# A due date for the readers of PSUM, more tiles for split weights, and a stricter VectorE in the planner of a two-layer block

## The chip, the cores and the metric

One core of one Trainium2 chip runs the whole program. The metric is device microseconds (us) of one execution; the figure for a kernel is the median of its runs. "The profile" is the page written from one profiled execution, "the trace" the record behind it, from which further rows can be asked.

## The reference

Two layers of a block that mixes tokens in four ways at once. There are 256 latent tokens and 256 context tokens of width 1024; layer 0 computes both, layer 1 the latent ones alone (its context tokens serve only as keys and values).

```python
for l in range(DEPTH):
    h = modulate(rms_norm(x, norm_gain[l, 0]), mod[:, 0], mod[:, 1])
    hc = modulate(rms_norm(ctx, norm_gain[l, 0]), mod_c[:, 0], mod_c[:, 1])
    pl = split_cols(h @ w_in[l])
    pc = split_cols(hc @ w_in[l])
    a_l, a_c = gqa_branch(...)
    b_l, b_c = retention_branch(...)
    c_l, c_c = mla_branch(...)
    d_l, d_c = diff_branch(...)
    y = gated_merge([a_l, b_l, c_l, d_l], pl[13], w_branch[l], w_out[l])
    x = x + mod[:, 2][:, None] * y
    h2 = modulate(rms_norm(x, norm_gain[l, 1]), mod[:, 3], mod[:, 4])
    x = x + mod[:, 5][:, None] * swiglu(h2, w_ffn_in[l], w_ffn_out[l])
    ...
```

`mod` comes from a matrix of 1024 by 6144 weights for each layer (`adaln`). `gated_merge` sums, over the branches, sigmoid gates times the branch's projection, and projects the sum once more. `swiglu` has 2816 hidden channels. All is float32.

## The kernel before

**The arithmetic.** Every matmul against weights, and most of the attention, is made of three: each operand is split into a high part rounded to fp32r and a low part, the rest, and the products hi·hi, hi·lo and lo·hi are summed in PSUM. For weights, `Weights._split` takes a piece of a loaded tile `wraw`, copies it to `whi` (`cp`, a CAST), and VectorE subtracts: `wlo = wraw - whi`. The same pair of steps splits the transposed probabilities (`pthi`, `ptlo`, out of the PSUM tile `ps_t`), stacked queries and keys (`sthi`, `stlo`), normalised activations (`hhi`, `hlo`) and branch outputs (`ohi`, `olo`).

**The stages** in the order of time: modulation of the first norm and transposes of the input; layer 0's input projection, with its four branches' attention laid between its matmuls; layer 0's merge (gates, branch projections and output projection); its FFN; the same for layer 1. The modulation vectors of later stages are summed on VectorE (`macc`: one weight row block times a column of `sil`, added on, in chains of SCALAR_TENSOR_TENSOR) beside the earlier stages; `MODS` says beside which. In the merge `glog` and `sig` hold the gates; `glog<-glog,ps_s` multiplies a gate into a branch projection that stands in PSUM, and frees that PSUM bank. In the FFN, `fsig` does the same for silu(gate) times up.

**The order.** Nothing is emitted directly. A `Recorder` collects every operation with what it depends on, and `schedule` plans them with a cost for each: `backward` places every operation as late as it may go, which gives its priority `prio` (the lowest first); `forward` goes through time and lets each engine take, among its ready operations, the one of lowest `prio` that `allowed` admits. `emit` (line 432) then issues all of them in that order, so that all rows of the trace bear one line. Engines work through their own lists strictly in order: an operation that waits holds up all behind it on that engine.

Three rules of `forward` matter here. `allowed` refuses an operation whose new tiles would exceed a limit: 8 banks of PSUM, by uses `PS_LIMITS = {"acc":5,"s":8,"t":3,"v":3}`; 73 tiles in the pool "u"; and of these at most `W_LIMIT = 34` for `whi` and `wlo`, 17 pairs (`w_tiles`, line 536). The priority does not know PSUM: an operation that would free a bank counts by when its result is wanted. And `worth` decides between engines where an operation has alternatives: `cp` (line 576) is ScalarE's first and may go to VectorE; `scale_rows` (line 580) is VectorE's first and may go to ScalarE or GpSimd. An engine that is not the first takes the operation only if it would end it sooner than the other, with a margin added to its own end:

```python
if e != ops[i][0][0][0]:
    mine += MARGIN[e]
```

With -0.3 for VectorE it takes a copy even if it would end it up to 0.3 us (of the planner's time) later than ScalarE.

Of the kernel before, what the change touches and what calls it, by code (L numbers as in the profile page):

```python
# [33 lines left out]
WRAW_LIMIT = 4  # L34
MRAW_LIMIT = 4
SLACK = 1
MARGIN = {"vector": -0.3, "scalar": -0.1, "gpsimd": 0}
W_LIMIT = 34
MOD_LAG = 600
REL_LAG = 200  # L40
DECAY_LAG = 0
# [22 lines left out]
class Recorder:  # L64
# [221 lines left out]
    def forward(self, users, deps, prio):  # L286
        ops = self.ops
        n = len(ops)
        tiles = {}
        caps = {}  # L290
        for nm, (f, l, c) in self.span.items():
            tiles[nm] = [[tag for tag, _ in self.tag[nm]], f, l, c, False]
            caps.update(self.tag[nm])
        prof = {t: np.zeros(n + 1, dtype=np.int32) for t in caps}
        for tags, f, l, c, _ in tiles.values():
            for tag in tags:
                prof[tag][f:l + 1] += 1
        live = dict.fromkeys(caps, 0)
        for t, c in caps.items():
            assert prof[t].max() <= c, (t, prof[t].max(), c)  # L300
        done = [False] * n
        issued = [False] * n
        low = 0
        free = dict.fromkeys(self.ENGINES, 0.0)
        left = [len(d) for d in deps]
        est = [0.0] * n
        pick = [0] * n
        heaps = {e: [] for e in self.ENGINES}
        ends = []
        wait = [(est[i], i) for i in range(n) if not left[i]]  # L310
        heapq.heapify(wait)
        now = 0.0
        order = []
        self.times = {}

        held = 0.0

        def begin(v):
            return max(now, held) if v[6] else now

        def allowed(i):
            new = {}
            for nm in ops[i][2]:
                t = tiles[nm]
                if not t[4]:
                    for tag in t[0]:
                        new.setdefault(tag, []).append(t[1])
            for tag, firsts in new.items():
                k = len(firsts)
                if live[tag] + k > caps[tag]:  # L330
                    return False
                f = max(firsts)
                if f > low and prof[tag][low:f].max() + k > caps[tag] - (SLACK if caps[tag] > 16 else 0):
                    return False
            return True

        def worth(e, i, p):

            mine = next(begin(v) + v[4] for v in ops[i][0] if v[0] == e)
            if e != ops[i][0][0][0]:  # L340
                mine += MARGIN[e]
            for v in ops[i][0]:
                if v[0] != e:
                    t = max(begin(v), free[v[0]]) + v[4]
                    if t < mine:
                        t += sum(ops[j][0][0][4] for q, j in heaps[v[0]] if (q, j) < (p, i) and not issued[j])
                        if t < mine:
                            return False
            return True
        while len(order) < n:  # L350
            while wait and wait[0][0] <= now + 1e-9:
                _, i = heapq.heappop(wait)
                for v in ops[i][0]:
                    heapq.heappush(heaps[v[0]], (prio[i], i))
            while ends and ends[0][0] <= now + 1e-9:
                _, i = heapq.heappop(ends)
                done[i] = True
                for nm in ops[i][2]:
                    t = tiles[nm]
                    t[3] -= 1  # L360
                    if t[3] == 0:
                        for tag in t[0]:
                            live[tag] -= 1
                            prof[tag][low:t[2] + 1] -= 1
                while low < n and done[low]:
                    low += 1
            nxt = wait[0][0] if wait else 1e18
            if ends:
                nxt = min(nxt, ends[0][0])
            for e in self.ENGINES:  # L370
                h = heaps[e]
                while h and issued[h[0][1]]:
                    heapq.heappop(h)
                if not h:
                    continue
                if free[e] > now + 1e-9:
                    nxt = min(nxt, free[e])
                    continue
                skipped = []
                found = -1  # L380
                while h and len(skipped) < 200:
                    p, i = heapq.heappop(h)
                    if issued[i]:
                        continue
                    if allowed(i) and (len(ops[i][0]) == 1 or worth(e, i, p)):
                        found = i
                        break
                    skipped.append((p, i))
                for x in skipped:
                    heapq.heappush(h, x)  # L390
                if found < 0:
                    continue
                i = found
                issued[i] = True
                for nm in ops[i][2]:
                    t = tiles[nm]
                    if not t[4]:
                        t[4] = True
                        for tag in t[0]:
                            live[tag] += 1  # L400
                            if t[1] > low:
                                prof[tag][low:t[1]] += 1
                pick[i] = next(x for x, v in enumerate(ops[i][0]) if v[0] == e)
                v = ops[i][0][pick[i]]
                end = begin(v) + v[4]
                free[e] = end
                if v[6]:
                    held = end
                self.times[i] = now
                if e == "sync":  # L410
                    free[e] = max(end, now + 0.565)
                heapq.heappush(ends, (end + (DMA_LAT if e == "sync" else 0.0), i))
                order.append(i)
                for u in users[i]:
                    left[u] -= 1
                    w = ops[u][0][0][0]
                    lat = 0.0 if e == "tensor" == w else v[5] + self.EXTRA[w]
                    est[u] = max(est[u], end + lat)
                    if not left[u]:
                        heapq.heappush(wait, (est[u], u))  # L420
                nxt = min(nxt, free[e])
            if nxt >= 1e18:
                raise RuntimeError("schedule stuck")
            now = max(now, nxt)
        return order, pick
# [89 lines left out]
class Builder:  # L515
# [20 lines left out]
    def w_tiles(self):  # L536
        pair = self.u(F32R, "whi"), self.u(F32R, "wlo")
        for t in pair:
            self.nc.own(t, ("u", NU), ("w", W_LIMIT))
        return pair  # L540
# [1724 lines left out]
```

## Time and profile before

| what | value |
|---|---|
| runs | 1776.82, 1778.41, 1778.12 us; median 1778.12 |
| profiled execution | 1776.79 us |
| its span, by the trace | 1774.9 us (1.9 us lie outside it) |
| TensorE busy | 1726.4 us, 97% of the span |
| VectorE busy | 1334.3 us, 75% |
| ScalarE busy | 846.9 us, 48% |
| GpSimd busy | 58.7 us, 3% |
| mean granted clock of TensorE | 0.993 of full speed |

PE is TensorE's matmuls, PEld its weight loads, DVE is VectorE, ACT ScalarE, POOL GpSimd, SP the engine that issues most transfers. In a row `out<-in` names the tiles; numbers of buffers are left out. "Idle before" is the time that an engine stood still ahead of an instruction, with what released it. Matmul durations overlap their neighbours; what one costs is the distance from its start to the next start.

### The profile page before, as it was taken

What the parts mean: (1) busy time and instruction counts of PE and PEld (TensorE: products, weight loads), DVE (VectorE), ACT (ScalarE), POOL (GpSimd) and SP (SyncE); (2) the same over time, 40 slices, a digit from 0 to 9 for tenths busy, and PEclk for the clock granted to TensorE, in tenths of its full rate; (3) what the DMA queues carried; (4) which work ended last, traced back from release to release, by engine and by line L of the source; (5) the groups of instructions that cost most, each with busy time, mean ns of one, the idle gap of its engine ahead of it and who ended that gap; (6) DMA issues with size and microseconds to landing.
All of it is one profiled execution on the core that took longest, in us unless ns stands there. A gap on an engine that the chain in (4) does not pass through costs nothing. (4 is left out here: it accounts for less than half of the span.)

```text
span 1774.9 us, 30925 instructions
## 1 busy us (share of the span) xinstructions
PE 1726.4 (97%) x11510; PEld 1564.5 (88%) x11510; DVE 1334.3 (75%) x3055; ACT 846.9 (48%) x2014; POOL 58.7 (3%) x89
## 2 busy tenths in 40 slices
PE   7999999999899999999999999998999899999999
PEld 5988999998687887878888789997999789999999
DVE  5899999888989678786436533989989796786563
ACT  4378665556423333532222322666655544564441
POOL 0010000001010000000000000000000100000000
PEclk9999999999999999999999999999999999999999
DMA  9413113334546465355226522342234576756451
GB/s 310 165 45 117 50 35 110 93 96 125 166 154 193 151 214 166 108 189 189 83 72 197 189 89 75 110 118 63 72 93 129 148 222 190 233 161 183 138 187 62
DMA packets 204345, 243.72 MB, mean 137 GB/s; under 512 B 9994, under 2 KB 183204, under 8 KB 204196
## 3 DMA queue, kind: packets, MB, share of 16 engines
q1 hardware_dynamic: 203840, 241.61, 44.4%
q8 instruction: 90, 1.47, 0.3%
q14 instruction: 59, 0.48, 0.1%
q10 hardware_dynamic: 356, 0.14, 0.0%
HBM read 224.15 MB, written 1.05 MB: 127 GB/s over the span
## 5 line engine op out<-in xcount | busy, mean ns | idle before, releaser
L432 ACT CAST whi<-wraw 128x512 fp32r<-128x512 f32 (+3 forms) x630 | 361.1, 605 | 353.6 <-PE ps_acc L432 160.3
L432 DVE TENSOR_TENSOR wlo<-wraw,whi 128x512 fp32r<-128x512 f32 (+4 forms) x674 | 436.4, 668 | 120.2 <-PE ps_acc L432 65.7
L432 PE MATMUL ps_acc<-hhi,wlo 128*128 128x256 f32 (+1 forms) x864 | 292.7, 339 | 8.9 <-DVE wlo L432 6.1
L432 PE MATMUL ps_acc<-hlo,whi 128*128 128x256 f32 (+1 forms) x864 | 289.7, 335 | 0.2
L432 PE MATMUL ps_acc<-hhi,whi 128*128 128x256 f32 (+1 forms) x864 | 289.4, 335 | 0.0
L432 PE MATMUL ps_acc<-whi,hhi 128*128 128x256 f32 (+2 forms) x896 | 262.5, 293 | 1.2 <-ACT x L432 0.9
L432 PE MATMUL ps_acc<-wlo,hhi 128*128 128x256 f32 (+2 forms) x896 | 254.5, 284 | 0.3 <-DVE wlo L432 0.3
L432 PE MATMUL ps_acc<-whi,hlo 128*128 128x256 f32 (+2 forms) x896 | 254.6, 284 | 0.0
L432 PEld LDWEIGHTS ps_acc<-hhi,wlo 128*128 128x128 f32 x864 | 164.6, 191 | 28.4 <-DVE wlo L432 7.7
L432 PEld LDWEIGHTS ps_acc<-hlo,whi 128*128 128x128 f32 x864 | 164.6, 190 | 17.3 <-DVE hlo L432 0.7
L432 PEld LDWEIGHTS ps_acc<-hhi,whi 128*128 128x128 f32 x864 | 164.7, 191 | 14.9
L432 PEld LDWEIGHTS ps_acc<-whi,hhi 128*128 128x128 f32 x896 | 171.2, 191 | 3.0 <-ACT x L432 1.3
L432 PEld LDWEIGHTS ps_acc<-wlo,hhi 128*128 128x128 f32 x896 | 171.4, 191 | 1.0 <-DVE wlo L432 0.5
L432 PEld LDWEIGHTS ps_acc<-whi,hlo 128*128 128x128 f32 x896 | 171.0, 191 | 0.0
L432 DVE SCALAR_TENSOR_TENSOR macc<-mraw,sil,macc 128x512 f32<-128x512 f32 x224 | 157.8, 752 | 15.7 <-DMA mraw<-in_w_mod_dram 13.4
L432 PE MATMUL ps_acc<-fhi,wlo 128*128 128x256 f32 (+1 forms) x396 | 127.5, 322 | 0.0
L432 PE MATMUL ps_acc<-flo,whi 128*128 128x256 f32 (+1 forms) x396 | 126.2, 319 | 0.0
L432 PE MATMUL ps_acc<-fhi,whi 128*128 128x256 f32 (+1 forms) x396 | 126.1, 319 | 0.0
L432 PE MATMUL ps_s<-hhi,wlo 128*128 128x512 f32 (+1 forms) x352 | 119.2, 339 | 1.3 <-ACT hhi L432 1.3
L432 PE MATMUL ps_s<-hlo,whi 128*128 128x512 f32 (+1 forms) x352 | 119.1, 338 | 0.5 <-DVE hlo L432 0.5
L432 PE MATMUL ps_s<-hhi,whi 128*128 128x512 f32 (+1 forms) x352 | 119.0, 338 | 0.0
L432 PE MATMUL ps_s<-ohi,wlo 128*128 128x512 f32 (+1 forms) x256 | 88.4, 345 | 6.7 <-DVE glog L432 6.6
(247 smaller groups left out, 3563.5 us busy)
## 6 DMA issues: line engine op xcount, KB each, us to landing
wraw<-in_w_in_dram SPq DMA_DIRECT2D x124, 512.0 KB, 4.6
mraw<-in_w_mod_dram SPq DMA_DIRECT2D x96, 512.0 KB, 4.8
wraw<-in_w_ffn_in_dram SPq DMA_DIRECT2D x88, 512.0 KB, 3.5
wraw<-in_w_ffn_out_dram SPq DMA_DIRECT2D x40, 512.0 KB, 4.6
wraw<-in_w_branch_dram SPq DMA_DIRECT2D x32, 512.0 KB, 3.6
wraw<-in_w_out_dram SPq DMA_DIRECT2D x16, 512.0 KB, 4.9
stb<-sthi SPq DMA_DIRECT2D x36, 128.0 KB, 2.3
std<-stlo SPq DMA_DIRECT2D x24, 128.0 KB, 2.3
```

What stands on the lines that cost most here:

```text
L432: getattr(getattr(self.nc, eng), m)(*a, **k)
```

## The change

Three parts, all in the planner; no operation is added or removed.

1. **A due date.** In `forward`, an operation that is not TensorE's and touches a tile in PSUM is a `reader`. When it becomes ready, its priority becomes the smaller of its own and the time at which it became ready plus `DUE = 12.0` us (on the scale of the priorities, `horizon` being the start of the backward plan).
2. **More tiles for split weights.** `W_LIMIT` goes from 34 to 40, that is from 17 to 20 pairs, out of the same 73.
3. **VectorE's margin** goes from -0.3 to 0.3: it takes a copy of ScalarE's only where it would end it more than 0.3 us sooner.

```diff
-MARGIN = {"vector": -0.3, "scalar": -0.1, "gpsimd": 0}
-W_LIMIT = 34
+DUE = 12.0
+MARGIN = {"vector": 0.3, "scalar": -0.1, "gpsimd": 0}
+W_LIMIT = 40
...
         held = 0.0
+        prio = list(prio)
+        horizon = -min(prio)
+        reader = [o[0][0][0] != "tensor" and any(x.startswith("ps_") for x in o[2]) for o in ops]
...
             while wait and wait[0][0] <= now + 1e-9:
                 _, i = heapq.heappop(wait)
+                if reader[i]:
+                    prio[i] = min(prio[i], est[i] - horizon + DUE)
                 for v in ops[i][0]:
                     heapq.heappush(heaps[v[0]], (prio[i], i))
```

What the planner emits with it, at three places. The emitting line is 432 before and 438 in the changed kernel; "x3" is three in a row.

**Place 1: VectorE at the start of layer 0's merge** (around 479 us of the trace). `macc` are sums of modulation vectors, `glog<-glog,ps_s` the readers of PSUM. Before:

```order
L432 TENSOR_TENSOR wlo<-wraw,whi 128x512
L432 SCALAR_TENSOR_TENSOR macc<-mraw,sil,macc 128x512 x3
L432 TENSOR_TENSOR wlo<-wraw,whi 128x512
L432 SCALAR_TENSOR_TENSOR macc<-mraw,sil,macc 128x512 x8
L432 SCALAR_TENSOR_TENSOR glog<-glog,ps_s 128x512 x3
L432 TENSOR_TENSOR glog<-glog 128x512
L432 TENSOR_TENSOR wlo<-wraw,whi 128x512
L432 SCALAR_TENSOR_TENSOR glog<-glog,ps_s 128x512 x2
```

Eight `macc` stand ahead of the first reader. In the changed kernel:

```order
L438 SCALAR_TENSOR_TENSOR glog<-glog,ps_s 128x512
L438 TENSOR_TENSOR olo<-o,ohi 128x512
L438 SCALAR_TENSOR_TENSOR glog<-glog,ps_s 128x512
L438 TENSOR_TENSOR wlo<-wraw,whi 128x512
L438 TENSOR_TENSOR olo<-o,ohi 128x512
L438 TENSOR_TENSOR wlo<-wraw,whi 128x512
L438 TENSOR_TENSOR olo<-o,ohi 128x512 x3
L438 TENSOR_TENSOR wlo<-wraw,whi 128x512
L438 SCALAR_TENSOR_TENSOR glog<-glog,ps_s 128x512
L438 TENSOR_TENSOR olo<-o,ohi 128x512
L438 SCALAR_TENSOR_TENSOR glog<-glog,ps_s 128x512
L438 TENSOR_TENSOR wlo<-wraw,whi 128x512 x4
```

The first four readers of the merge stand ahead of the run of `macc`, which begins with the next row.

**Place 2: VectorE in layer 1's attention of the GQA branch** (around 1205 us), with the numbers of the tiles. `mk` are normalised keys of another branch, which touch no PSUM; `ptlo`, `o` and `v` read PSUM. Before:

```order
L432 TENSOR_TENSOR mk_2825<-x_3087,sm_3093 128x4x64
L432 CAST pthi_3072<-ps_t_3071 128x512
L432 TENSOR_TENSOR mk_2827<-x_3087,sm_3093 128x4x64
L432 TENSOR_TENSOR ptlo_3073<-ps_t_3071,pthi_3072 128x512
L432 TENSOR_TENSOR mk_2829<-x_3088,sm_3093 128x4x64
L432 TENSOR_TENSOR mk_2831<-x_3088,sm_3093 128x4x64
```

VectorE casts `pthi_3072` itself, and `mk` stand between. In the changed kernel:

```order
L438 TENSOR_TENSOR ptlo_3073<-ps_t_3071,pthi_3072 128x512
L438 TENSOR_TENSOR o_2933<-ps_v_3036,pvl_3037 64x256
L438 TENSOR_TENSOR t2_3048<-x_3040,ropeg_2727 128x512
L438 TENSOR_TENSOR v_3151<-ps_acc_3110,v_3151 128x4x64
L438 TENSOR_TENSOR ptlo_3076<-ps_t_3074,pthi_3075 128x512
L438 TENSOR_TENSOR v_3152<-ps_acc_3110,v_3152 128x4x64
L438 CAST pthi_3083<-ps_t_3082 128x512
```

`pthi_3072` has gone to ScalarE, and the readers of PSUM follow one another with the `mk` behind them. Over the program VectorE's `pthi<-ps_t` casts of 128x512 go from 33 to 7, its `x<-ps_acc` copies of 128x512 from 12 to 3, its `sthi<-ps_t` of 128x512 from 12 to 8, and its `whi<-wraw` casts of 128x512 from 30 to 48, ScalarE having the rest; GpSimd's `p<-p,sm` of 128x512 go from 7 to 14. TensorE has the same instructions as before.

**Place 3: TensorE in layer 0's attention of the GQA branch** (around 150 us). `ps_acc<-whi,cqhi` and its two companions are projections of another branch; `ps_t<-ident,p` transposes probabilities, `ps_v` multiplies them into the values, `ps_s` are scores. Before:

```order
L432 MATMUL ps_v<-pthi,v 128x256
L432 MATMUL ps_acc<-whi,cqhi 128x256
L432 MATMUL ps_acc<-wlo,cqhi 128x256
L432 MATMUL ps_acc<-whi,cqlo 128x256
L432 MATMUL ps_v<-ptlo,v 64x256 x2
L432 MATMUL ps_v<-pthi,v 128x256
L432 MATMUL ps_t<-ident,p_583 128x128 x4
L432 MATMUL ps_acc<-whi,cqhi 128x256
```

Projections stand between the steps of the attention. In the changed kernel:

```order
L438 MATMUL ps_v<-pthi,v 128x256
L438 MATMUL ps_t<-ident,p_583 128x128
L438 MATMUL ps_v<-ptlo,v 64x256 x2
L438 MATMUL ps_v<-pthi,v 128x256
L438 MATMUL ps_s<-sthi 128x512
L438 MATMUL ps_s<-stlo,sthi 128x512
L438 MATMUL ps_s<-stb 128x512
L438 MATMUL ps_s<-std,stb 128x512
L438 MATMUL ps_t<-ident,p_585 128x128 x4
```

Here 57 matmuls of the attention follow one another without a projection.

## Rows read from the trace of the kernel before

**Rows 1.** The page's first part: busy time, share of the span, instructions.
```profile
PE 1726.4 (97%) x11510; PEld 1564.5 (88%) x11510; DVE 1334.3 (75%) x3055; ACT 846.9 (48%) x2014; POOL 58.7 (3%) x89
```

**Rows 2.** Windows: stretch, its us, busy PE PEld DVE ACT POOL, granted clock, DMA.
```profile
100.00:175.00 75.00, 73.09 (x490) 64.67 (x489) 70.67 (x176) 62.42 (x162) 8.45 (x20) 1.00 0.34 96
175.00:450.00 275.00, 270.91 (x2111) 260.36 (x2111) 251.39 (x656) 173.95 (x443) 15.17 (x20) 1.00 0.29 83
...
725.00:775.00 50.00, 47.19 (x282) 39.43 (x281) 44.69 (x103) 23.29 (x85) 0.00 (x0) 1.00 0.44 138
775.00:1175.00 400.00, 400.00 (x2125) 343.04 (x2124) 219.03 (x454) 136.51 (x322) 8.99 (x16) 1.00 0.40 125
1175.00:1300.00 125.00, 117.37 (x873) 108.71 (x872) 119.36 (x297) 89.51 (x200) 4.53 (x4) 0.99 0.26 75
...
1375.00:1450.00 75.00, 64.46 (x470) 61.21 (x469) 62.97 (x174) 36.59 (x86) 5.24 (x10) 0.93 0.53 160
```

**Rows 3.** Timelines of DVE, then of PE, about 480 us; then windows.
```profile
478.85 5.39 DVE L432 SCALAR_TENSOR_TENSOR macc<-mraw,sil,macc 128x512 f32<-128x512 f32 x8
484.15 1.88 DVE L432 SCALAR_TENSOR_TENSOR glog<-glog,ps_s 128x512 f32<-128x512 f32 x3
...
484.89 0.79 PE L432 MATMUL ps_s<-ohi,wlo 128*128 128x512 f32 x1 [5.32 <-DVE glog L432]
...
484.90:488.50 3.60, 3.60 (x9) 2.83 (x10) 3.60 (x7) 0.62 (x1) 0.00 (x0) 0.50 0.58 154
575.00:600.00 25.00, 25.00 (x112) 20.71 (x111) 16.50 (x26) 5.92 (x10) 3.24 (x3) 1.00 0.45 141
```

**Rows 4.** Waits of PE, 1375 to 1450 us (total, times, longest); then windows.
```profile
PE ps_acc L432 <- DVE wlo L432: 5.5, 3, 2.5
...
PE ps_s L432 <- DVE glog L432: 1.3, 1, 1.3
...
1375.00:1400.00 25.00, 21.59 (x164) 20.82 (x162) 16.81 (x44) 10.72 (x19) 1.77 (x6) 0.93 0.29 77
1400.00:1425.00 25.00, 19.26 (x139) 17.62 (x140) 24.13 (x68) 14.94 (x38) 3.48 (x4) 0.97 0.70 220
```

**Rows 5.** Waits of PE, 1175 to 1300 us; then a window.
```profile
PE ps_v L432 <- DVE o L432: 2.7, 1, 2.7
PE ps_t L432 <- DVE ptlo L432: 2.4, 3, 1.9
...
1200.00:1225.00 25.00, 19.19 (x119) 15.92 (x118) 23.69 (x70) 13.72 (x34) 0.00 (x0) 0.93 0.08 22
```

**Rows 6.** Waits of PE, 100 to 450 us.
```profile
PE ps_t L432 <- DVE otok L432: 0.9, 1, 0.9
PE ps_t L432 <- DVE x L432: 0.8, 1, 0.8
```

**Rows 7.** Timeline of DVE about 762 us; then waits of PE, 725 to 775 us.
```profile
762.20 11.34 DVE L432 SCALAR_TENSOR_TENSOR macc<-mraw,sil,macc 128x512 f32<-128x512 f32 x17
...
PE ps_acc L432 <- DVE fsig L432: 1.3, 1, 1.3
```

**Rows 8.** Groups of instructions by form, DVE, ACT, POOL: busy us, mean ns.
```profile
L432 DVE CAST pthi<-ps_t 128x512 fp32r<-128x512 f32 x33 | 22.5, 684 | 2.8 <-PE ps_t L432 2.6
...
L432 DVE CAST whi<-wraw 128x512 fp32r<-128x512 f32 x30 | 12.6, 420 | 8.3 <-DMA wraw<-in_w_in_dram 4.8 <-PE ps_acc L432 3.5
...
L432 DVE TENSOR_TENSOR mk<-x,sm 128x256 f32<-128x256 f32 x16 | 6.1, 412 | 0.0
...
L432 DVE TENSOR_SCALAR p<-p,sm 128x512 f32<-128x512 f32 x24 | 11.5, 478 | 0.2
...
L432 ACT CAST whi<-wraw 128x512 fp32r<-128x512 f32 x578 | 340.9, 620 | 340.9 <-PE ps_acc L432 149.8 <-PE ps_s L432 56.3 <-DMA wraw<-in_w_in_dram 41.5
...
L432 ACT CAST pthi<-ps_t 128x512 fp32r<-128x512 f32 x67 | 38.5, 586 | 17.2 <-PE ps_t L432 13.1 <-PE ps_v L432 3.1 <-DVE o L432 0.4
...
L432 POOL TENSOR_TENSOR p<-p,sm 128x512 f32<-128x512 f32 x7 | 7.7, 1101 | 136.1 <-DVE sm L432 136.1
```

## The prediction

> **What bounds the kernel now.** I read the page's first part, then windows by stage, then the waits of TensorE in the stages that are not full, then the timeline around each. TensorE is busy in 1726.4 of 1774.9 us [rows 1]; 48.5 us are idle. Where it is full, as from 775 to 1175 us (400.00 of 400.00) [rows 2], nothing that the planner does for VectorE can gain, since TensorE's work is the same before and after. So the question is only where the 48.5 us lie and who holds them. Five stretches have them: 100 to 175 lacks 1.9, 175 to 450 lacks 4.1, 725 to 775 lacks 2.8, 1175 to 1300 lacks 7.6, 1375 to 1450 lacks 10.5 [rows 2]; and one wait by itself, 5.32 us at 479 us [rows 3]. The other 16 us (48.5 less these 32.2) are spread over the other stages, the start and the end among them, and are left as they are. In all six places the waits name VectorE most, with a reader of PSUM (`glog`, `o`, `ptlo`, `fsig`) or a `wlo`. VectorE is also the busy one there: 70.67 of 75 us, 119.36 of 125 [rows 2].
>
> A wait costs a second time. After the 5.32 us, nine matmuls of 512 columns took 3.60 us at a granted clock of 0.50, that is at 1.2 instead of 2.4 GHz; at full clock 112 of the same take 25.00 us [rows 3], 0.223 each, so nine take 2.0: 1.6 us were lost. TensorE had stood still before the clock fell.
>
> **The sum.** All terms are against the profiled execution, 1776.8 us. The median of the runs is 1.3 above it, and 1.3 is added at the end. About 0.2%, 3.5 us, is what a measurement of this kernel can tell from no change.
>
> *(a) The merge of layer 0.* Eight `macc` take 5.39 us on VectorE from 478.85, and the `glog` that frees a bank starts at 484.15, when TensorE has stood still for nearly as long [rows 3]. In the new order (place 1) the first four `glog` stand ahead of the run. The wait goes with its clock: 5.3 + 1.6 = **-6.9** (at least 5, if another 1.9 us of `wlo` or `olo` stay ahead of it). What is late next is `macc`, which no stage near it wants.
>
> *(b) 1375 to 1450.* Three waits for `wlo` make 5.5 us and one for `glog` 1.3 [rows 4]. VectorE has less to do ahead of them: 26 casts `pthi` of 684 ns (17.8 us) and 9 copies `x`, taken at the same price (6.2 us), leave it over the program, while 18 casts `whi` of 420 ns (7.6 us) come to it [rows 8]; the PSUM readers go by their due date, and 20 pairs let `wlo` be made earlier. I take both waits as gone, and the clock of the two windows that hold the `wlo`, (0.07 + 0.03) × 25 = 2.5 us [rows 4]: **-9.3**. At most all goes: 10.5 of idle time and 0.07 × 75 = 5.2 of clock [rows 2], -15.7. At least nothing goes.
>
> *(c) 1175 to 1300.* Waits for `o` 2.7 and `ptlo` 2.4, the longest 1.9, and a window of 25 us at 0.93, which costs 1.75 [rows 5]. Place 2 shows four `mk` of 412 ns [rows 8] that stood between the readers of PSUM and now stand behind, and the cast on ScalarE. I take 2.7 + 1.9 + 1.75 = **-6.3**; at most 7.6 + 1.75 = -9.4, at least nothing.
>
> *(d) 100 to 450.* 6.0 us are idle in many waits of under 1 us. Of these `otok` 0.9 and `x` 0.8 are VectorE's work behind PSUM [rows 6]: **-1.7**, between 0 and -6.0.
>
> *(e) 725 to 775.* Seventeen `macc` in a row take 11.34 us ahead of `fsig`, and TensorE waits 1.3 for it [rows 7]. The due date lifts `fsig` over them: **-1.3**, between 0 and -2.8.
>
> *(f) Work that moves.* ScalarE gets the 35 copies, at 586 each 20.5 us, and gives up 18 casts of 620, 11.2 [rows 8]; it is at 48% [rows 1], so this costs nothing while its idle time covers it. SP issues the same transfers, and the tiles that a delayed `macc` holds come free some 5 us later, and no wait of TensorE read here names a transfer [rows 3 to 7]: nothing, and if the cover were gone, some of (g).
>
> *(g) New waits.* No row shows what the readers' precedence pushes back: `mk`, `macc`, scalings of `p`. GpSimd gets 7 more of `p`, at 1101 ns against VectorE's 478 [rows 8], and if TensorE waited for each, 7 × 0.62 = 4.4. The upper bound is two more stretches like 1200 to 1225, where 5.8 us are idle and 1.75 lost to the clock [rows 5]: 15.1. Below nothing is left out, since the gains are counted above. I take **+4**, by the nearer row.
>
> -6.9 - 9.3 - 6.3 - 1.7 - 1.3 + 4 = -21.5. 1776.8 - 21.5 = 1755.3, and with 1.3 the median is **1757**.
>
> **The rivals.**
>
> *Slower: the fillers are used up too early.* With 20 pairs and earlier readers the projections run ahead of the attention, and nothing is left to lay between its steps: place 3 shows 57 matmuls of layer 0's GQA attention without a projection. TensorE then goes at the pace of VectorE's and ScalarE's chain from scores to `ptlo`, as from 1200 to 1225 us [rows 5]. Two such stretches, one in each layer, cost 15.1. If then only (a), (e) and the longest `wlo` wait of 2.5 [rows 4] are gained, 10.7, the sum is +4.4: 1776.8 + 4.4 + 1.3 = 1782.5. It decides from about 14 us of new waits on with these gains. For it: VectorE has only 4.3 us free of 75 in that stage of layer 0 [rows 2]. Against: it is VectorE that loses work there, and TensorE had 1.9 us idle with the same chain.
>
> *No effect.* A due date of 12 us after becoming ready is longer than the waits that it should remove (5.32 at most) [rows 3], so most readers keep the place that they had, and what is gained in one place is lost in (g): within 3.5 us, 1778. Against: place 1 shows the readers moved.
>
> *ScalarE becomes the bound.* From 100 to 175 us it is busy for 62.42 of 75 [rows 2], 12.6 free. If all 35 copies fell there, 20.5 - 12.6 = 7.9 us would be over, and the forecast would become 1757 + 8 = 1765. The Trainium skill has a rule that speaks against the third part: "TensorEngine Tiling (Array Packing)", section "PSUM Bottleneck", says that the copying out of PSUM can become the limit and that ScalarE and VectorE should both be used for it. By that rule the 26 casts should stay shared; no row here shows TensorE waiting long for ScalarE. Only a part of the 35 lies in that stage, and a cast from PSUM takes VectorE 684 ns and ScalarE 586, while one from SBUF takes 420 against 620 [rows 8]: the exchange of the two kinds makes both engines cheaper.
>
> *Better than forecast.* Everything that (a) to (e) bound goes and nothing comes: 6.9 + 15.7 + 9.4 + 6.0 + 2.8 = 40.8, so 1736.0, and 1737 with 1.3. It asks that no stage be limited by VectorE any more, though it stays at 119.36 less some 10 of 125 [rows 2]. Half of the step from the forecast to it gives 1747.
>
> **How the numbers follow.** Forecast (1747 to 1767) 0.55; ScalarE the bound, which is still faster, 0.15; better than 1747, 0.10; no effect 0.10; slower 0.10. So faster by over 0.2% (below 1774.6) 0.80, within it 0.10, slower (above 1781.7) 0.10. The range is 1740 to 1776: downwards it takes in most of "better", upwards all the cases of (g) in which new waits take nearly all of the gain; it leaves out the slower case, most of no effect and the last of "better".
>
> **What the profile would show.** If right: no wait for `glog` of over 1 us in layer 0's merge and no 0.5 clock behind it (a); `wlo` waits between 1375 and 1450 under 1 us together (b); `o` and `ptlo` gone from the waits about 1206 and 1219 us (c); VectorE busy for about 1318 us (1334.3 - 17.8 - 6.2 + 7.6), ScalarE for about 856 (846.9 + 20.5 - 11.2); TensorE idle for some 27 us rather than 48.5. It would be wrong if waits for `ps_t` or `ps_v` of over 5 us together stood in either GQA attention (the fillers), if they named ScalarE's `pthi` (ScalarE the bound), or if new waits stood where `macc`, `mk` or `p` are wanted, in stretches that are full now.

## The result, and the profile after

The changed kernel takes 1749.99 us (median of 4 runs, 1748.84 to 1751.57); beside it the kernel before took 1777.47 (4 runs). The ratio is 0.9846, with a 95% interval of 0.9829 to 0.9863: 27.5 us faster, where 21.5 had been forecast. The profiled execution took 1750.57 us, its span is 1748.5, against 1774.9 before: 26.4 less.

The first part of the page of the changed kernel answers to [rows 1]:

```profile
PE 1716.3 (98%) x11510; PEld 1559.5 (89%) x11510; DVE 1313.7 (75%) x3020; ACT 857.7 (49%) x2041; POOL 70.5 (4%) x97
```

TensorE's idle time went from 48.5 to 32.2 us (1748.5 - 1716.3), 16.3 less. The other 10.1 us are in its busy time, 1726.4 before, for the same 11510 matmuls. About 7 of them go with the granted clock, whose mean rose from 0.993 to 0.997 (worked out in the last section); what the other 3 are is not shown. VectorE lost 20.6 us and ScalarE gained 10.8.

Windows of the changed kernel, in the columns of [rows 2]; two are moved along with the work, which comes some 10 and 25 us earlier there:

```profile
100.00:175.00 75.00, 73.69 (x502) 65.76 (x501) 68.38 (x176) 65.58 (x168) 10.41 (x21) 1.00 0.34 95
175.00:450.00 275.00, 273.36 (x2118) 262.03 (x2117) 245.29 (x648) 178.49 (x453) 17.09 (x23) 1.00 0.31 86
715.00:765.00 50.00, 45.56 (x272) 39.13 (x271) 44.82 (x103) 26.08 (x91) 1.09 (x1) 0.97 0.40 131
1175.00:1300.00 125.00, 122.75 (x940) 114.97 (x939) 123.16 (x300) 94.82 (x215) 9.58 (x8) 1.00 0.28 83
1350.00:1425.00 75.00, 68.78 (x531) 66.50 (x530) 64.92 (x199) 44.17 (x112) 5.09 (x10) 0.95 0.49 142
```

Four of the five are fuller than their rows before; the FFN's norm of layer 0 (715 to 765) is emptier: 4.4 us idle, where 2.8 were.

The waits of TensorE over the whole span, the longest in all, of the changed kernel (total, times, longest):

```profile
PE ps_t L438 <- DMA ident<-in_ident_dram: 4.4, 1, 4.4
PE ps_acc L438 <- DVE hlo L438: 3.2, 2, 2.0
PE ps_v L438 <- DVE ptlo L438: 3.0, 4, 1.4
PE ps_t L438 <- ACT modrows L438: 2.9, 3, 1.7
PE ps_t L438 <- DMA xtok<-in_ctx_dram: 2.4, 2, 1.9
PE ps_acc L438 <- DVE wlo L438: 2.2, 4, 0.9
```

Before the change the list began like this:

```profile
PE ps_s L432 <- DVE glog L432: 6.6, 2, 5.3
PE ps_acc L432 <- DVE wlo L432: 6.4, 5, 2.5
```

`glog`, `fsig` and `o`, which stood among the waits before (6.6, 1.3 and 2.7 us), are not among them now. `hlo` is new at this length (0.5 us before), and it is in the stretch that became emptier.

To split the gain, two points that every version passes are read from TensorE's timeline: the first projection of layer 1, and the transposes that end the program. Before:

```profile
1112.78 0.34 PE L432 MATMUL ps_acc<-whi,hhi 128*128 128x384 f32 x1
...
1769.73 1.18 PE L432 MATMUL ps_t<-ident,xT 128*128 128x128 f32 x8
```

In the changed kernel:

```profile
1104.73 0.34 PE L438 MATMUL ps_acc<-whi,hhi 128*128 128x384 f32 x1
...
1743.33 1.18 PE L438 MATMUL ps_t<-ident,xT 128*128 128x128 f32 x8
```

Layer 0 gives 8.0 us, all after it 18.4 (26.4 - 8.0). The table at the end of the experiments gives these two figures for every version.

### The profile page after: what moved, and what is told of

Same layout as the page of the kernel before. It is cut to its first block, busy times and chain, and to the rows that moved or that the text cites. A ratio compares the mean times of both kernels' runs of the same rounds, so it can differ in the third digit from the quotient of the medians.

```text
span 1748.5 us, 31005 instructions
## 1 busy us (share of the span) xinstructions
PE 1716.3 (98%) x11510; PEld 1559.5 (89%) x11510; DVE 1313.7 (75%) x3020; ACT 857.7 (49%) x2041; POOL 70.5 (4%) x97
## 5 line engine op out<-in xcount | busy, mean ns | idle before, releaser
L438 ACT CAST whi<-wraw 128x512 fp32r<-128x512 f32 (+2 forms) x613 | 351.8, 607 | 348.2 <-PE ps_acc L438 155.3
```

The source lines that it names most:

```text
L438: getattr(getattr(self.nc, eng), m)(*a, **k)
```

## Experiments

Theory A was that of the prediction: the due date puts readers of PSUM ahead of work that nobody waits for, and the margin takes load from VectorE. The rivals were that the lighter load (B) or the additional pairs of tiles (C) carry the gain; later, that the last part of it belongs to no part of the change (F).

### Each part alone

Due date alone: `MARGIN` and `W_LIMIT` stay as before.

```diff
-MARGIN = {"vector": 0.3, "scalar": -0.1, "gpsimd": 0}
-W_LIMIT = 40
+MARGIN = {"vector": -0.3, "scalar": -0.1, "gpsimd": 0}
+W_LIMIT = 34
```

> Only the due date; margin -0.3 and 17 pairs as before. In the order of this kernel the first four readers of the merge stand ahead of the macc run, and VectorE has 5 of the pthi casts, fewer than in the whole change (7). Theory A (the due date carries the gain, by putting readers of PSUM ahead of work in SBUF): 1755 to 1762 us, that is over half of the 27.5 us; the 5.3 us wait for glog at the merge of layer 0 is gone, and the waits for o and ptlo in layer 1's GQA attention too. Rival B (VectorE's lighter load by the margin carries it): over 1768. Rival C (the 20 pairs carry it, wlo made earlier): over 1768, with the waits for wlo of layer 1 still there.

Measured: 1754.86 us, ratio 0.9885 (0.9866 to 0.9904), 20 us less, at the fast edge of A's range (0.1 us under it). The waits for `glog` and `o` are gone, as A said, but one of 3.0 us for `ptlo` is left in layer 1's GQA attention, which A did not expect. The first part of its page:

```profile
PE 1716.2 (98%) x11510; PEld 1560.9 (89%) x11510; DVE 1341.5 (77%) x3075; ACT 838.5 (48%) x1995; POOL 57.7 (3%) x88
```

VectorE is busy for longer than before the change (1341.5 against 1334.3) and the kernel is 20 us faster: here the order of the work made the gain, not the amount of VectorE's. Rival B falls as the only cause.

Margin alone, in the kernel before:

```diff
-MARGIN = {"vector": -0.3, "scalar": -0.1, "gpsimd": 0}
+MARGIN = {"vector": 0.3, "scalar": -0.1, "gpsimd": 0}
```

> Only the margin 0.3; no due date, 17 pairs. VectorE has 2 pthi casts in place of 33, but six macc still stand ahead of the first glog of layer 0's merge and 17 ahead of fsig in its FFN. Theory A: the two waits in those places stay (about 4 and 1 us); some of layer 1's go; 1768 to 1776 us. Rival B: 1752 to 1762. Rival C: within 3.5 us of before.

Measured: 1759.32 us, ratio 0.9908 (0.989 to 0.9927), 16 us less. That is more than theory A gave it (1768 to 1776); rival B's range held it. So the two parts alone make 20 and 16 us, more together than the whole change: they relieve in part the same waits. Of its waits of TensorE:

```profile
PE ps_s L432 <- DVE glog L432: 6.6, 2, 5.4
PE ps_acc L432 <- DVE wlo L432: 4.2, 3, 2.8
...
PE ps_acc L432 <- DVE fsig L432: 1.7, 1, 1.7
```

The waits at layer 0's merge and FFN are as they were, as theory A said, and layer 0 gains 0.7 us. The gain lies after layer 0: 11.5 us in the profiled execution, which was the slowest of its six runs, 5.1 us above the median.

Tiles alone, in the kernel before:

```diff
-W_LIMIT = 34
+W_LIMIT = 40
```

> Only 20 pairs in place of 17; no due date, margin -0.3. Eight macc still stand ahead of the first glog of layer 0's merge. Theory A and rival B: within 5 us of before, 1772 to 1782 us. Rival C: under 1768, with the waits for wlo between 1375 and 1450 us gone.

Measured: 1771.57 us, ratio 0.9977 (0.9966 to 0.9989). A gain of 4 to 5 us, 0.4 us under the range that A and B gave, and far from C. The waits for `wlo` are 4.6 us in all, where 6.4 were; layer 0 even ends 5.1 us later.

### Two parts of three

The changed kernel without the tiles:

```diff
-W_LIMIT = 40
+W_LIMIT = 34
```

> The whole change without the 20 pairs (17 as before). Theory A: within 4 us of the whole change, 1748 to 1756 us. Rival C: over 1760, the wlo waits of layer 1 back.

Measured: 1755.59 us, ratio 0.9887 (0.9867 to 0.9908). The margin adds nothing to the due date alone. The time is at the top of A's range, and the tiles seem to be worth 6 us here, in layer 1.

The changed kernel without the due date (the lines on `reader` go too):

```diff
-                if reader[i]:
-                    prio[i] = min(prio[i], est[i] - horizon + DUE)
```

> The whole change without the due date. Six macc stand ahead of the first glog of layer 0's merge, 18 ahead of fsig. Theory A (the due date orders VectorE; the margin lightens it; in layer 1's attention either relieves the same waits, in layer 0's merge only the due date does): 1755 to 1763 us; up to the end of layer 0 within 4 us of before, with waits for glog and fsig of together over 5 us; layer 1's attention shorter by 10 us or more. Rival B (parts add up: -16 for the margin, -4 for the tiles, measured alone): 1753 to 1757. Rival D (without the due date the 20 pairs do harm, as in layer 0 of the run with the tiles alone): over 1765.

Measured: 1768.38 us, ratio 0.9961 (0.9947 to 0.9974). Worse than the margin alone by 9 us: rival D was right, A and B (here: that the parts add up) were wrong. In layer 0 what A said holds: the waits for `glog` are 5.4 us again, and layer 0 ends 2.2 us later than before.

The changed kernel with the margin of before:

```diff
-MARGIN = {"vector": 0.3, "scalar": -0.1, "gpsimd": 0}
+MARGIN = {"vector": -0.3, "scalar": -0.1, "gpsimd": 0}
```

> The whole change without the margin (-0.3 as before). VectorE keeps 27 of the 33 pthi casts. Theory A: layer 0 gains as in the whole change (some 8 to 10 us at the start of layer 1), layer 1 less, since VectorE's load there is that of before: 1755 to 1762 us. Rival B (parts add up: -20 and -4): 1750 to 1755.

Measured: 1755.64 us, ratio 0.9884 (0.987 to 0.9898), as A said. So the due date alone, with the margin, and with the tiles make 0.9885, 0.9887 and 0.9884. Only the three together make 0.9846. Either there is an effect that needs all three, or the last 6 us come from something that none of them is.

### Which readers the due date serves

The due date only for the readers of the merges and the FFN:

```diff
-        reader = [o[0][0][0] != "tensor" and any(x.startswith("ps_") for x in o[2]) for o in ops]
+        reader = [o[0][0][0] != "tensor" and any(x.startswith("ps_") for x in o[2])
+                  and any(x.startswith(("glog", "sig", "fsig")) for x in o[2]) for o in ops]
```

> The whole change, but the due date holds only for readers that touch glog, sig or fsig: those of the merges and the FFN. All else as in the run without the due date. Theory A: against that run the waits for glog at layer 0's merge (5.4 us and its half clock) and for fsig go, 7 to 9 us less; the attention stages as there. Against the whole change it is missing what the due date does in the attention stages: 1750 to 1756 us. Rival E (the due date works mainly through the attention's readers): within 3 us of the run without the due date.

Measured: 1759.34 us, ratio 0.9904 (0.989 to 0.9918): 9 us less than without a due date, as A said (7 to 9), and 9 more than the whole change. The range that A gave as a time, 1750 to 1756, was missed by 3 us; 7 to 9 less than the 1768.38 of that run would have been 1759 to 1761. Layer 0 gains 7.5 us, nearly what the whole change gains there.

The complement, all readers but these:

```diff
+                  and not any(x.startswith(("glog", "sig", "fsig")) for x in o[2]) for o in ops]
```

> The whole change, but readers that touch glog, sig or fsig get no due date; those of the attention and the norms do. Six macc stand ahead of the first glog of layer 0's merge again. Theory A: the wait for glog there (5 us and its clock) is back, layer 1's attention gains as in the other kernels with a due date (9 to 12 us): 1758 to 1765 us. Rival (the gates' part of the due date is worth nothing by itself): within 3 us of the change, 1747 to 1753.

Measured: 1768.13 us, ratio 0.9944 (0.9927 to 0.9962). The wait for `glog` in layer 0's merge is back at 5.4 us, and layer 0 gains only 2.0:

```profile
PE ps_s L439 <- DVE glog L439: 6.4, 2, 5.4
```

The profiled execution gains 11.9 us in layer 1, but it was a short one among its runs (1762.76). The median is 3 us above A's range, and within 0.3 us of that of the margin and the tiles without any due date (1768.38): beside these two, a due date for the attention's and the norms' readers alone gains nothing that the time shows.

### The new wait, taken away

At the FFN's norm of layer 0 `xn` reads PSUM (the broadcast of the norm's factors), so it has a due date. VectorE's timeline in the changed kernel:

```profile
725.13 3.22 DVE L438 SCALAR_TENSOR_TENSOR xn<-xT,sm,ps_t 128x256 f32<-128x256 f32 x8 [0.65 <-PE ps_t L438]
728.26 0.16 DVE L438 TENSOR_TENSOR modT<-ps_t,featT 128x8 f32<-128x8 f32 x1
728.34 0.48 DVE L438 SCALAR_TENSOR_TENSOR hlo<-xn,modT,hhi 128x256 fp32r<-128x256 f32 x1
```

All eight `xn` run before the first `hlo`, and TensorE's rows that wait for it are these:

```profile
728.87 0.40 PE L438 MATMUL ps_acc<-hlo,whi 128*128 128x256 f32 x1 [1.12 <-DVE hlo L438]
737.19 0.39 PE L438 MATMUL ps_acc<-hlo,whi 128*128 128x256 f32 x1 [2.03 <-DVE hlo L438]
```

Taking `xn` out of the readers:

```diff
+                  and not any(x.startswith("xn") for x in o[2]) for o in ops]
```

> The whole change, but xn, which reads PSUM at the FFN's norm of layer 0, gets no due date. In the order the first hlo stands behind four xn again, as before the change, and not behind eight. Theory: the two waits for hlo (3.2 us together) about 730 us go, 2 to 4 us less than the whole change: 1746 to 1749 us. Rival: another operation of the norm ends last there (modrows, hhi), within 1.5 us of the whole change.

Measured: 1753.85 us, ratio 0.9876 (0.9863 to 0.9889): not 3 us better than the change but 4 to 5 worse. Yet the step did what it was for: no wait for `hlo` over 0.2 us is left, and layer 0 gains 11.6 us, 3.6 more than the change. Layer 1 gives it all back: it gains 11.3 where the change gains 18.4, with a wait of 3.3 us for one `wlo` near 1394 us:

```profile
1393.98 0.48 PE L439 MATMUL ps_acc<-hhi,wlo 128*128 128x256 f32 x1 [3.27 <-DVE wlo L439]
```

Both forecasts, 1746 to 1749 and within 1.5 us of the change, were missed. The edit does reach into layer 1: of the 32 `xn` that read `ps_t`, 16 belong to layer 1's first norm (1099 to 1113 us in the changed kernel), and there too `xn` and `hlo` alternate now. No operation near 1394 us lost its due date. Whether the new order there comes from those 16 or from what the planner has in hand after layer 0 was not tried.

### Is the last part of the gain the change's own?

The same change with a margin between the two that were measured:

```diff
-MARGIN = {"vector": 0.3, "scalar": -0.1, "gpsimd": 0}
+MARGIN = {"vector": 0.15, "scalar": -0.1, "gpsimd": 0}
```

> The whole change with a margin of 0.15 in place of 0.3. VectorE has 9 pthi casts (7 in the change), glog stands ahead of macc as in the change. Theory F (the last 6 us of the change, all in layer 1's attention, are an accident of the order that the three numbers happen to give, and no effect of the tiles or the margin by themselves): 1752 to 1760 us, layer 0 as in the change within 3 us. Rival (a smooth effect of the margin: at -0.3 1755.6, at 0.3 1750): 1750 to 1753.

Measured: 1765.53 us, ratio 0.993 (0.9913 to 0.9946). With -0.3 it was 1755.64 and with 0.3 it is 1749.99; a smooth effect falls. Theory F was right in kind and too small in size (1752 to 1760). Layer 0 gains 6.8 us, near the change's 8.0; layer 1 gains 3.0. Two of TensorE's waits in this kernel near the end of layer 1's attention:

```profile
1394.31 0.39 PE L438 MATMUL ps_acc<-hhi,wlo 128*128 128x256 f32 x1 [2.92 <-DVE wlo L438]
...
1412.72 0.55 PE L438 MATMUL ps_s<-sthi 128*128 128x256 f32 x1 [4.74 <-DMA sthi<-stlo]
```

One `wlo` and one transfer that moves a stacked tile came late in this order. They make 7.7 of the 11.6 us by which TensorE idles longer than in the changed kernel (43.8 us against 32.2).

### A later due date

```diff
-DUE = 12.0
+DUE = 30.0
```

> The whole change with DUE = 30 in place of 12. In the order the four first glog still stand ahead of every macc, and the first hlo of the FFN's norm stands behind four xn, not eight. Theory G (a reader needs only to pass work whose result is wanted much later, as macc; a later due date passes less work that is wanted soon): the waits for hlo go (3 us) and the merge stays as in the change: 1741 to 1749 us. Rival (a due date of 30 us is too late for the attention, whose waits come back): 1755 to 1765.

Measured: 1744.34 us, ratio 0.982 (0.9802 to 0.9838), as theory G said. VectorE's timeline at the norm, in this kernel:

```profile
724.85 1.26 DVE L438 SCALAR_TENSOR_TENSOR xn<-xT,sm,ps_t 128x256 f32<-128x256 f32 x3
726.69 0.49 DVE L438 SCALAR_TENSOR_TENSOR hlo<-xn,modT,hhi 128x256 fp32r<-128x256 f32 x1 [0.58 <-ACT hhi L438]
727.09 0.48 DVE L438 SCALAR_TENSOR_TENSOR xn<-xT,sm,ps_t 128x256 f32<-128x256 f32 x1
```

`hlo` comes after three `xn`, and TensorE waits for it for 0.2 us in all. Layer 0 gains 11.5 us. In layer 1 one wait of 4.75 us for a `wlo` is back (at 1384.72).

The last run changed all three numbers of the changed kernel:

```diff
-DUE = 12.0
-MARGIN = {"vector": 0.3, "scalar": -0.1, "gpsimd": 0}
-W_LIMIT = 40
+DUE = 30.0
+MARGIN = {"vector": 0.8, "scalar": -0.1, "gpsimd": 0}
+W_LIMIT = 42
```

> DUE = 30, a margin of 0.8 for VectorE and 21 pairs. VectorE keeps 1 pthi cast. Theory G with a lighter VectorE: 1737 to 1747 us. Rival (ScalarE becomes the bound with the copies that it gets): over 1750, with waits for ScalarE's pthi or x in layer 0's attention.

Measured: 1735.41 us (1733.68 to 1736.23), ratio 0.9765 (0.975 to 0.9781): 40 us less than before, better than both kernels, and 1.6 us faster than theory G's range (1737 to 1747). Its page's first part and two of its windows:

```profile
PE 1706.4 (98%) x11510; PEld 1555.6 (90%) x11510; DVE 1297.5 (75%) x2973; ACT 880.4 (51%) x2093; POOL 69.9 (4%) x92
```

```profile
100.00:175.00 75.00, 74.85 (x519) 67.75 (x518) 66.80 (x175) 67.89 (x174) 9.44 (x20) 1.00 0.28 75
1175.00:1300.00 125.00, 124.05 (x972) 118.58 (x971) 118.16 (x297) 93.54 (x213) 4.16 (x4) 1.00 0.25 73
```

The rival, ScalarE as the bound, falls where it was strongest: from 100 to 175 us ScalarE is busy for 67.89 of 75 us, more than VectorE, and TensorE misses 0.15 us.

### The table

Time that a version is ahead of the one before (profiled executions, us) at the first projection of layer 1, and what it gains from there to the last transposes. "Gates due" says whether the readers of the merges and the FFN have a due date.

| version | gates due | ratio | layer 0 | after it |
|---|---|---|---|---|
| margin alone | no | 0.9908 | 0.7 | 11.5 |
| tiles alone | no | 0.9977 | -5.1 | 8.5 |
| margin, tiles | no | 0.9961 | -2.2 | 10.5 |
| all, no due date for gates | no | 0.9944 | 2.0 | 11.9 |
| due date alone | yes | 0.9885 | 10.3 | 12.6 |
| due date, margin | yes | 0.9887 | 9.3 | 12.0 |
| due date, tiles | yes | 0.9884 | 8.7 | 13.8 |
| all, due date for gates only | yes | 0.9904 | 7.5 | 7.0 |
| all, margin 0.15 | yes | 0.993 | 6.8 | 3.0 |
| all, no due date for `xn` | yes | 0.9876 | 11.6 | 11.3 |
| **the change** | yes | 0.9846 | 8.0 | 18.4 |
| all, DUE = 30 | yes | 0.982 | 11.5 | 20.3 |
| DUE = 30, margin 0.8, 42 | yes | 0.9765 | 15.8 | 25.7 |

Three profiled executions lie far from the median of their version: that of the margin alone 5.1 us above it, of the gates only 2.8 above, of no due date for the gates 5.4 below. Their rows are uncertain by as much.

The column for layer 0 splits by one condition: with a due date for the gates 6.8 to 15.8, without it -5.1 to 2.0. These are terms (a) and (e) of the prediction together, since the gates' due date holds for the merge and the FFN, and the cause is shown. The last column has no such condition: any version gains something there, most of them 7 to 14, and which part it has does not order them.

## Why the prediction was right

The direction and its main places were right; the time came out 7 us below the forecast and inside the range. The terms below make 23 of the 26.4 us between the two profiled executions; the other 3 were not traced.

- **(a) The merge of layer 0**: forecast -6.9. From the timelines the output projection of layer 0 starts 10.1 us earlier (683.46 and 673.34); 3.0 of these are idle time that went from 100 to 450 (below), so (a) gave about 7. The runs show its cause as stated: TensorE waits for `glog` for 4.2 to 6.6 us in the five versions without a due date for the gates (the kernel before among them), and in the nine with it no wait for `glog` is listed. The granted clock of the stretch went from 0.99 to 1.00.
- **(b) 1375 to 1450**: forecast -9.3; it gave about 6: idle time 10.5 to 6.2, and the clock from 0.93 to 0.95 of 75 us, 1.5 more. The waits for `wlo` there are 1.4 us together, where the prediction's sign was under 1. The reason was half wrong. I read the waits for `wlo` as VectorE's load. Its timeline before the change, ahead of the first of them (TensorE resumed at 1393.42), shows otherwise:

```profile
1387.96 0.69 DVE L432 TENSOR_TENSOR wlo<-wraw,whi 128x512 fp32r<-128x512 f32 x1 [0.41 <-PE ps_acc L432]
1389.52 0.69 DVE L432 COPY x<-ps_acc 128x512 f32<-128x512 f32 x1 [0.87 <-PE ps_acc L432]
...
1392.68 0.69 DVE L432 TENSOR_TENSOR wlo<-wraw,whi 128x512 fp32r<-128x512 f32 x1
```

VectorE stood idle for 0.87 us ahead of the copy, and `wlo` was behind that in the list, with the work on `x`. Its `whi` was there: the trace shows no cast of a `whi` on either engine from 1387.54 to 1392.68. VectorE was busy for 16.81 us of the 25 around it [rows 4]. So for this first wait it was the order, not the load. The other two `wlo` waits, 1.8 and 1.1 us, lie between 1400 and 1425, where VectorE is busy for 24.13 of 25 us [rows 4]; there the load stays a possible reason. Nor does the change remove such waits for good: of the fourteen versions only the change and the due date alone have no single wait for a `wlo` of over 2 us between 1370 and 1434; in the others it is 2.2 to 4.75 us (3.3 without `xn`'s due date, 2.92 with a margin of 0.15, 3.1 in the fastest). Nothing in the prediction tells the change from those others, so that it escapes the wait is luck. Whether the limit on tiles or the priorities kept these `wlo` back was not tried by itself.
- **(c) 1175 to 1300**: forecast -6.3; idle time went from 7.6 to 2.3, and the mean clock from 0.99 to 1.00, about 1.2 more: -6.6. The waits for `o` and `ptlo` are gone. The cause is borne out in part. In this window TensorE idles for 6.2 to 7.6 us in the five versions in which the attention's readers have no due date, and for 0.9 to 5.8 in eight of the nine in which they have one; the ninth is the due date alone, with 7.0. So in these traces the due date helps there beside one of the other parts and not by itself, and how much varies. The window with the due date alone, and with all but the gates' due date:

```profile
1175.00:1300.00 125.00, 118.03 (x888) 111.66 (x887) 121.70 (x298) 84.01 (x190) 4.16 (x4) 0.95 0.24 71
1175.00:1300.00 125.00, 119.54 (x922) 113.10 (x921) 121.75 (x298) 93.07 (x209) 9.88 (x9) 1.00 0.28 81
```

- **(d) 100 to 450**: forecast -1.7; idle time went from 6.0 to 3.0 (1.3 and 1.6 in the two windows). Undersized, since I counted only two of its waits.
- **(e) The FFN of layer 0**: forecast -1.3; the wait for `fsig` is gone, but the stretch lost 2.1 us (from 10.1 ahead at the output projection to 8.0 at layer 1). This is (g)'s new wait, `hlo`, 3.2 us. I had not named it: (g) spoke of `mk`, `macc` and `p`, and none of these appears in the waits.
- **(f)**: VectorE 1313.7 us and ScalarE 857.7, forecast 1318 and 856. TensorE's waits for ScalarE's `pthi` rose only from 0.6 to 1.3 us, so 0.7 us is what shows of the copies that moved. One transfer did stand among the waits before in (b)'s window, `stlo` with 0.7 us, though (f) says that none was read.
- **(g)**: forecast +4; the new wait is 3.2 us, in (e).
- **Not in the sum**: the stretch at layer 1's FFN norm, which the prediction left as it is, gave 2.6. Before and after:

```profile
1575.00:1600.00 25.00, 23.20 (x179) 22.80 (x178) 22.40 (x59) 16.15 (x46) 0.00 (x0) 0.93 0.49 149
```

```profile
1550.00:1575.00 25.00, 24.09 (x199) 23.68 (x199) 23.34 (x62) 16.47 (x48) 0.00 (x0) 1.00 0.48 150
```

Idle time went from 1.8 to 0.9 us, and the clock gave back 0.07 of 25 us, 1.75.

The sign of 27 us of idle time was worked out wrongly: it takes all 21.5 us off the idle time, though 5.9 of them (1.6, 2.5 and 1.75) were clock. 48.5 - 15.6 = 32.9 is what the terms give, and 32.2 was measured.

What the prediction did not see is how much of the sum in layer 1 is luck. Its terms (b) and (c) came near, but a margin of 0.15 would have had the same diff but for one number, nearly the same argument, and 1765.53 us. Both rivals of weight fell by the windows: the fillers did not run out (from 100 to 175 us TensorE is idle for 1.3 us, not 1.9, with the 57 matmuls in a row), and ScalarE did not become the bound, at 65.58 of 75 us there. The rule of the Trainium skill ("TensorEngine Tiling (Array Packing)", section "PSUM Bottleneck") is to use both ScalarE and VectorE for the copies out of PSUM. In the last version one of the 100 `pthi` casts of 128x512 was VectorE's, and it is the fastest. In no version do TensorE's waits for ScalarE's `pthi` come to more than 2.2 us together, and in the last none is listed. VectorE still takes all 100 `ptlo` out of the same PSUM tiles, so both engines read PSUM even there. How much that margin by itself gave was not tried.

The rival "no effect" said that 12 us is too late for waits of 5. A due date of 30 us, later still, is faster. So the due date need not be shorter than the wait; it has to come before the date of the work ahead. With 30 the first four `glog` still stand ahead of the run of `macc`, whose own date is later still in this plan.

## What to carry to other kernels

A planner that ranks work by when its result is wanted does not know what an operation holds while it waits. A reader of PSUM holds a bank, and a date of its own, generous enough not to pass work that is wanted soon, lets it pass the work that nobody waits for; here that removed a wait of 3.6 to 5.4 us in layer 0's merge in every version that had it. Where an order comes from list scheduling, a gain of under one per cent of the time from a changed constant needs the neighbouring constants beside it: here a margin between two measured ones lost 10 us against one and 16 against the other, with two late operations making nearly 8 us of idle time. And when an operand comes late from an engine, look first for idle time of that engine ahead of it: if it is there, as at 1389 us, the order of its list is at fault and not its load.

## What the runs showed of the hardware

TensorE's busy time, for the same matmuls, fell by 10.1 us beside 16.3 us of idle time (the change), and by 20.0 beside 21.5 in the last version (1726.4 to 1706.4; idle 48.5 to 27.0). The mean granted clock explains a part. It was 0.993 before, 0.997 in the change and 0.999 in the last version; as an estimate from these and the spans, 12.4, 5.2 and 1.7 us were lost to it (0.007 of 1774.9, 0.003 of 1748.5, 0.001 of 1733.4). So the clock gave back some 7 us in the change, near the 5.9 that the prediction's terms had in them, and some 11 in the last version. What the other 3 and 9 us of busy time are is not shown. The ends of matmuls in the record are modelled, and records overlap (from 1389 to 1390 us of the kernel before, matmuls of 128x256 start some 0.12 us apart and are 0.28 long), so short delays between starts can count as busy time.
